# Three 256-column products into one half of PSUM instead of one of 512 and one of 256, in the feature-major tiles of a two-layer decoder trunk

## The chip, the cores and the metric

The kernel runs on one core of one Trainium2 chip. The metric is the device time of one execution in microseconds (us). Each profile is one execution recorded by the hardware profiler. In its rows PE is TensorE's products (matmuls), PEld TensorE's loads of the stationary operand, DVE is VectorE, ACT is ScalarE, POOL is GpSimd, SP is SyncE, whose queue (SPq) issues most of the DMAs.

## The reference

A trunk of two pre-norm layers over 256 tokens of width 2048, all in float32. Cut to its products:

```python
h = x                                             # 256 x 2048
h = h + chunked_gmlp(rmsnorm(h, a_norm), ...)     # u, v = gelu(xn @ w_in); (u * mix(v)) @ w_out
h = h + conv_ffn(rmsnorm(h, f_norm[0]), ...)      # up to 2 x 5632, causal conv of width 3, silu(gate) * val, down
k, v, c = fox_shared_kv(h, kv_norm, w_kvf, ...)   # keys, values, cumulative log forget gates
h = h + forgetting_attention(rmsnorm(h, b_norm), w_qg, ..., k, v, c)
h = h + conv_ffn(rmsnorm(h, f_norm[1]), ...)
return rmsnorm(h, final_norm)
```

The weights are some 400 MB, and each is used once. A norm's gain is multiplied into the activations ahead of a product; its scale for each token is multiplied in behind it.

## The kernel before

**Precision.** A float32 product is made of three products of the type float32r. Each weight chunk is split on the core into a high part (`whi`, a rounding copy on ScalarE, L82) and a low part (`wlo`, the difference, on VectorE, L83). Each activation tile is kept as a high part in columns 0 to 255 and a low part in columns 256 to 511 of one buffer (`X1`, `X2`, `H`; T is 256, the number of tokens). The kernel forms high × high, high × low and low × high, and leaves low × low out.

**The stream.** `Stream` holds a list of all weight chunks (128 × 1024 float32, 512 KB) in the order of the work. `run` (L86) goes through it once: at chunk i it issues the DMA of chunk i+6 on SyncE's queue (`_load`, L62, four `raw` buffers), the split of chunk i+3 (`_split`, L73, four `whi` and four `wlo` buffers), then the products of chunk i, and then one step of each evicting generator that has been started (`advance`, L57). This order is written by hand, and each engine works through its own instructions in it. So the instruction that reads a tile's sums stands on its engine ahead of the split of chunk i+4.

**Two kinds of chunks.** In token-major chunks (`tok_block`, L215: `a_in_v`, `b_q`, `kvf_k`, `kvf_v`) the activations are the stationary operand and the weights move, 512 columns a product. In feature-major chunks (`feat_block`, L168: `a_in_u`, `a_out`, `up0`, `down0`, `b_g`, `b_out`, `up1`, `down1`) the weights are stationary. A chunk holds four blocks kt of 128 input features (j from 0 to 3) by two blocks m of 128 output features, so eight weight tiles of 128 × 128 in a high and a low version. A tile of output is two blocks m by 256 tokens. It takes 4 chunks where the input has 2048 features (KD = 16 blocks) and 11 where it has 5632 (KF = 44 blocks, `down`).

**The wide form.** For each weight tile the high part meets all 512 columns of the activations at once, and its results stand in the two halves of one PSUM bank: high × high in columns 0 to T, high × low in T to 2T. The low part meets columns 0 to T and is added to the lower half:

```python
mm(ps[:, m, :], w, xx[:, kt, :], kt == 0, kt == K - 1)      # L187, high part
mm(ps[:, m, :T], w, xx[:, kt, :T], False, False)            # L189, low part
```

That is 16 products a chunk: first 8 wide ones, then 8 of 256 columns; in the last chunk of a tile the low ones come first. Every product goes with its own weight load. A tile has two PSUM banks (`main_ps`, L155, three such pairs in rotation).

**Eviction.** The two halves have to be added. `scaled_sum` (L296; used by `u_done`, `up_done` and `g_done`) copies the upper half on ScalarE (L299), adds it to the lower on VectorE (L300) and multiplies by the norm's scale (L301). `residual` (L303; behind `a_out`, `down0` and `b_out`) adds the lower half to h (L307), then the upper (L308). `final` (L332; behind `down1`) does so for each block m (L339, L340).

**The last tile.** The last tile of `down1` has a form of its own (`last_block`, L194): for each m, four low products, four high ones with the low activations and four high ones with the high activations, all of 256 columns and into the lower half of the bank, 24 products a chunk. `final_tile` (L317) is called behind each m of the last chunk.

**Around it.** Attention is spread as small products (L615, L616, L631, L638 to L640; 16 heads) between the chunks of `kvf_v` and `b_g`; in `a_in_u` the spatial mixing (L446) stands between tiles. L382 is a warm-up of TensorE ahead of the first chunk, nine products of one identity tile with itself.

Of the kernel before, what the change touches and what calls it, by code (L numbers as in the profile page):

```python
# [10 lines left out]
F32 = mybir.dt.float32  # L11
# [121 lines left out]
def build(ctx, tc, d, out):  # L133
# [21 lines left out]
    def main_ps():  # L155
        return psum.tile([P, 2, 512], F32, name="ps", tag="ps", bufs=3)
# [8 lines left out]
    def mm(o, a, b, start, stop):  # L165
        nc.tensor.matmul(o, a, b, start=start, stop=stop, skip_group_check=True)  # L166

    def feat_block(src, x, K, done, last=None):  # L168


        if last:
            return last_block(src, x, K, done, last)
        box = {}
        n = K // 4
        for c in range(n):
            def mult(hi, lo, c=c):
                if c == 0:
                    box["ps"] = main_ps()
                ps, xx = box["ps"], x()
                parts = (hi, lo) if c < n - 1 else (lo, hi)  # L180
                for i, part in enumerate(parts):
                    for j in range(4):
                        kt = 4 * c + j
                        for m in range(2):
                            w = part[:, j * 256 + m * P:j * 256 + (m + 1) * P]
                            if part is hi:
                                mm(ps[:, m, :], w, xx[:, kt, :], kt == 0, kt == K - 1)  # L187
                            else:
                                mm(ps[:, m, :T], w, xx[:, kt, :T], False, False)  # L189
                if c == n - 1:  # L190
                    s.start(done(ps))
            s.chunk(src[c], mult)

    def last_block(src, x, K, done, last):  # L194
        box = {}
        n = K // 4
        for c in range(n):
            def mult(hi, lo, c=c):
                if c == 0:
                    box["ps"] = main_ps()  # L200
                ps, xx = box["ps"], x()
                for m in range(2):
                    for part, half in ((lo, 0), (hi, 1), (hi, 0)):
                        for j in range(4):
                            kt = 4 * c + j
                            mm(ps[:, m, :T], part[:, j * 256 + m * P:j * 256 + (m + 1) * P],
                               xx[:, kt, half * T:(half + 1) * T], part is lo and kt == 0,
                               half == 0 and part is hi and kt == K - 1)
                    if c == n - 1:
                        last(ps, m)  # L210
                if c == n - 1:
                    s.start(done(ps))
            s.chunk(src[c], mult)

    def tok_block(src, x, done, load=None, prep=None):  # L215
# [77 lines left out]
            for i in range(2):  # L293
                nc.vector.tensor_tensor(acc, acc, sq[:, i, :], op=OP.add)

    def scaled_sum(ps, a):  # L296

        t = small.tile([P, 2, T], F32, name="half", tag="half", bufs=2)
        nc.scalar.activation(t, ps[:, :, T:], AF.Copy)  # L299
        nc.vector.tensor_tensor(a, ps[:, :, :T], t, op=OP.add)  # L300
        nc.vector.tensor_tensor(a, a, rB[:, None, :].to_broadcast([P, 2, T]), op=OP.mult)  # L301

    def residual(p, gain):  # L303

        def done(ps):
            hh = h[:, 2 * p:2 * p + 2, :]
            nc.vector.tensor_tensor(hh, hh, ps[:, :, :T], op=OP.add)  # L307
            nc.vector.tensor_tensor(hh, hh, ps[:, :, T:], op=OP.add)  # L308
            for kt in (2 * p, 2 * p + 1):
                prep(X1, kt, gain)  # L310
            square_into_acc(p)
            yield
            if p == 7:
                yield from token_scale()
        return done
# [15 lines left out]

    def final(p, gain):  # L332

        def done(ps):
            kts = (2 * p, 2 * p + 1)
            if p < 7:
                sq = small.tile([P, 2, T], F32, name="sq", tag="sq", bufs=2)
                for m, kt in enumerate(kts):
                    nc.vector.tensor_tensor(h[:, kt, :], h[:, kt, :], ps[:, m, :T], op=OP.add)  # L339
                    nc.vector.tensor_tensor(h[:, kt, :], h[:, kt, :], ps[:, m, T:], op=OP.add)  # L340
                    nc.scalar.activation(sq[:, m, :], h[:, kt, :], AF.Square)
                if p == 0:
                    nc.vector.tensor_tensor(acc, sq[:, 0, :], sq[:, 1, :], op=OP.add)
                else:
                    for i in range(2):
                        nc.vector.tensor_tensor(acc, acc, sq[:, i, :], op=OP.add)
            for kt in kts:
                nc.scalar.activation(h[:, kt, :], h[:, kt, :], AF.Copy, scale=column(gain + kt))
            if p == 5:
# [83 lines left out]
        return done  # L433

    def u_done(p):
        def done(ps):
            X2, vt, wT, bB, _ = mlp_kept()
            u = ph.temp("u", [P, 2, T])
            scaled_sum(ps, u)
            yield  # L440
            nc.scalar.activation(u, u, AF.Gelu)
            mp = misc_ps()
# [20 lines left out]
        return ph.keep("H", [P, KF, 2 * T], F32R)  # L463

    def up_done(l, i):
        def done(ps):
            state["layer"] = l
            H = ffn_h()
            a = ph.temp("a", [P, 2, T])
            scaled_sum(ps, a)  # L470
            yield
            c = ph.temp("c", [P, 2, T])
            for m in range(2):
# [14 lines left out]

    def ffn(l, done):
        for i in range(KF):  # L490
            feat_block(d[f"up{l}"][4 * i:4 * i + 4], lambda: X1, KD, up_done(l, i))
        for p in range(8):
            feat_block(d[f"down{l}"][11 * p:11 * p + 11], ffn_h, KF, done(p), final_tile if l and p == 7 else None)


    def att(key):
        ph.open("att")
        shape = {"X2": [P, KD, 2 * T], "q": [P, NH, T], "k": [P, NH, T], "v": [P, 2, D],
                 "ccol": [P, 2, NH]}[key]
        return ph.keep(key, shape, F32R if key == "X2" else F32)  # L500
# [151 lines left out]
            yield  # L652

    def g_done(p):
        def done(ps):
            X2, o = att("X2"), att("q")
            gg = ph.temp("big", [P, 512], bufs=6).rearrange("p (a b) -> p a b", a=2)
            scaled_sum(ps, gg)
# [31 lines left out]
        if blk == 1:  # L690
            s.then(at_load=load_mix)
    for p in range(8):
        feat_block(d["a_in_u"][4 * p:4 * p + 4], lambda: X1, KD, u_done(p))
    for p in range(8):
        feat_block(d["a_out"][4 * p:4 * p + 4], mlp_x2, KD, residual(p, C_FNORM))
    ffn(0, lambda p: residual(p, C_BNORM))

    s.then(at_mult=lambda: s.start(kv_operand()))
# [6 lines left out]
    for blk in range(4):  # L705
        tok_block(d["kvf_v"][8 * blk:8 * blk + 8], lambda: att("X2"), v_evict(blk))
    for p in range(8):
        feat_block(d["b_g"][4 * p:4 * p + 4], lambda: X1, KD, g_done(p))
    for p in range(8):
        feat_block(d["b_out"][4 * p:4 * p + 4], lambda: att("X2"), KD, residual(p, C_FNORM + KD))  # L710
    ffn(1, lambda p: final(p, C_FINAL))
    s.run()
    ph.close()
# [60 lines left out]
```

## Time and profile before

| | us |
|---|---|
| median of 3 runs | 2244.74 (2244.12 to 2244.78) |
| the profiled execution | 2244.26 |
| its span | 2242.6 |
| TensorE, products busy | 2228.1 (12,546 products) |
| TensorE, weight loads busy | 1927.1 (12,546 loads) |
| VectorE busy | 1528.5 |
| ScalarE busy | 1193.5 |
| DMA, queue of the weights | 56.7% of 16 engines' span |

The granted TensorE clock was 0.998 of full speed over the span. A row of a group reads: line, engine, operation, out<-in, shapes, count | busy us, mean ns of one | idle time of the engine before them, and what ended it. A product's row shows its way through the array, and the next product starts before it has ended, so the rate is read from the starts. In the order-of-time view like products in succession are one row: start, duration from the first start to the last end, engine, line, what, count, and in brackets what the engine waited for ahead of it.

### The profile page before, as it was taken

How to read it: one execution, taken by the hardware profiler on the slowest of the kernel's cores; microseconds unless marked ns; L12 is line 12 of the kernel's file. 1: busy time of each engine (PE TensorE's matmuls, PEld its weight loads, DVE VectorE, ACT ScalarE, POOL GpSimd, SP SyncE). 2: the span in 40 equal slices, each digit the busy share in tenths (PEclk: the TensorE clock that was granted, in tenths of full speed). 3: DMA queues.
4: the chain of work that ended last, by engine and by line, in shares of the span. 5: the costliest groups of instructions: out<-in, count | busy, mean ns of one | idle time of the engine just before them, and what ended most of it. 6: DMA issues, size and time to landing. Idle time of an engine off the chain costs nothing.

```text
span 2242.6 us, 32429 instructions
## 1 busy us (share of the span) xinstructions
PE 2228.1 (99%) x12546; PEld 1927.1 (86%) x12546; DVE 1528.5 (68%) x2219; ACT 1193.5 (53%) x1625; POOL 19.2 (1%) x41
## 2 busy tenths in 40 slices
PE   9999999999999999999999999999999999999998
PEld 7888888888888888888788888888888888888887
DVE  6566777777777755557786567677777777765554
ACT  6544455555555544445444666446555555544442
POOL 0000000000000000000000110000000000000000
PEclk9999999999999999999999999999999999999999
DMA  8555555656555555555555555555555555565553
GB/s 299 180 187 173 191 190 191 192 190 189 193 191 188 190 183 191 197 190 177 171 183 188 166 168 179 187 189 193 191 188 188 191 191 191 190 196 188 191 190 127
DMA packets 116443, 422.12 MB, mean 188 GB/s; under 512 B 13232, under 2 KB 13376, under 8 KB 116032
## 3 DMA queue, kind: packets, MB, share of 16 engines
q1 hardware_dynamic: 115344, 417.93, 56.7%
q0 software_dynamic: 768, 2.10, 0.3%
q8 instruction: 98, 1.61, 0.3%
q14 instruction: 57, 0.47, 0.1%
q10 hardware_dynamic: 176, 0.02, 0.0%
HBM read 417.88 MB, written 2.11 MB: 187 GB/s over the span
## 4 chain that ended last, share of the span: by engine, by line
PE 99%; DVE 0%; DMA 0%; ACT 0%; SPq 0%; DVEq 0%; issue 0%
PE ps L166 97%; PE mp L446 0%; PE mp L530 0%; PE mp L616 0%; DMA raw<-a_in_v 0%; PE mp L631 0%; PE mp L639 0%; PE mp L640 0%; PE mp L615 0%; PE mp L638 0%; DVE h L362 0%; PE mp L329 0%; PE mp L277 0%; DVE wlo L83 0%; DVEq L768 0%; ACT whi L82 0%
## 5 line engine op out<-in xcount | busy, mean ns | idle before, releaser
L83 DVE TENSOR_TENSOR wlo<-raw,whi 128x1024 fp32r<-128x1024 f32 (+1 forms) x786 | 953.3, 1221 | 378.8 <-ACT whi L82 377.3
L82 ACT ACTIVATE whi<-raw 128x1024 fp32r<-128x1024 f32 (+1 forms) x786 | 822.1, 1054 | 383.2 <-PE ps L166 353.9
L166 PE MATMUL ps<-X,whi 128*128 128x512 f32 x3328 | 829.6, 396 | 0.0
L166 PEld LDWEIGHTS ps<-X,whi 128*128 128x128 f32 x3328 | 602.7, 188 | 120.4
L166 PEld LDWEIGHTS ps<-X,wlo 128*128 128x128 f32 x3328 | 426.2, 188 | 28.1
L166 PE MATMUL ps<-X,wlo 128*128 128x256 f32 x3328 | 430.7, 277 | 0.0
L166 PE MATMUL ps<-ffn_H,whi 128*128 128x512 f32 (+1 forms) x1496 | 355.4, 381 | 0.0
L166 PEld LDWEIGHTS ps<-ffn_H,whi 128*128 128x128 f32 x1496 | 258.7, 188 | 45.3
L299 ACT ACTIVATE half<-ps 128x512 f32<-128x512 f32 x104 | 62.1, 597 | 256.1 <-PE ps L166 256.1
L166 PEld LDWEIGHTS ps<-ffn_H,wlo 128*128 128x128 f32 x1408 | 184.6, 188 | 13.8 <-DVE h L324 0.3
L166 PE MATMUL ps<-ffn_H,wlo 128*128 128x256 f32 x1408 | 188.5, 277 | 0.2 <-DVE h L324 0.2
L300 DVE TENSOR_TENSOR ffn_a<-ps,half 128x512 f32<-128x512 f32 x88 | 60.9, 692 | 175.1 <-ACT half L299 175.1
L166 PE MATMUL ps<-whi,att_X 128*128 128x512 f32 x512 | 168.1, 400 | 0.0
L480 DVE SCALAR_TENSOR_TENSOR ffn_c<-ffn_a,col,ffn_c 128x255 f32<-128x255 f32 x352 | 162.1, 481 | 6.3
L166 PE MATMUL ps<-whi,X 128*128 128x512 f32 x512 | 162.8, 395 | 0.9 <-ACT whi L82 0.9
L476 ACT ACTIVATE ffn_c<-ffn_a,col 128x256 f32<-128x256 f32 x176 | 96.4, 595 | 47.3 <-DVE ffn_a L301 47.3
L166 PEld LDWEIGHTS ps<-whi,X 128*128 128x128 f32 x512 | 96.2, 188 | 21.9 <-ACT whi L82 1.5
L166 PEld LDWEIGHTS ps<-whi,att_X 128*128 128x128 f32 x512 | 96.3, 188 | 20.4
L166 PE MATMUL ps<-wlo,X 128*128 128x512 f32 x256 | 99.7, 390 | 1.0 <-DVE wlo L83 1.0
L166 PE MATMUL ps<-wlo,att_X 128*128 128x512 f32 x256 | 100.0, 391 | 0.0
L245 ACT ACTIVATE X<-h,col 128x256 fp32r<-128x256 f32 x64 | 29.0, 500 | 101.8 <-DVE h L308 99.5
L250 ACT ACTIVATE ffn_H<-ffn_c 128x256 fp32r<-128x256 f32 x88 | 36.7, 418 | 70.2 <-DVE ffn_c L484 70.2
(147 smaller groups left out, 1215.0 us busy)
## 6 DMA issues: line engine op xcount, KB each, us to landing
raw<-up SPq DMA_DIRECT2D x352, 512.0 KB, 3.8
raw<-down SPq DMA_DIRECT2D x176, 512.0 KB, 4.2
raw<-a_in_u SPq DMA_DIRECT2D x32, 512.0 KB, 3.6
raw<-a_out SPq DMA_DIRECT2D x32, 512.0 KB, 4.3
raw<-b_q SPq DMA_DIRECT2D x32, 512.0 KB, 4.2
raw<-kvf_k SPq DMA_DIRECT2D x32, 512.0 KB, 4.0
raw<-kvf_v SPq DMA_DIRECT2D x32, 512.0 KB, 3.6
raw<-b_g SPq DMA_DIRECT2D x32, 512.0 KB, 3.3
```

Of the source, the lines that this page charges most:

```text
L82: self.nc.scalar.activation(hi[:, :n], raw, AF.Copy)
L83: self.nc.vector.tensor_tensor(lo[:, :n], raw, hi[:, :n].bitcast(F32), op=OP.subtract)
L166: nc.tensor.matmul(o, a, b, start=start, stop=stop, skip_group_check=True)
L245: nc.scalar.activation(dst[:, kt, :T], h[:, kt, :], AF.Copy, scale=g)
L250: nc.scalar.activation(dst[..., :T], src, AF.Copy)
L299: nc.scalar.activation(t, ps[:, :, T:], AF.Copy)
L300: nc.vector.tensor_tensor(a, ps[:, :, :T], t, op=OP.add)
L476: nc.scalar.activation(c[:, m, :], a[:, m, :], AF.Identity, scale=w[2], bias=column(C_CONVB + l * 2 * KF + f))
L480: nc.vector.scalar_tensor_tensor(c[:, m, n:], a[:, m, :T - n], w[k], c[:, m, n:], op0=OP.mult, op1=OP.add)
```

## The change

`feat_block` gets a second form, and a list `wide` for each tile of those of its chunks that keep the first form.

In the narrow form the high part meets the two halves of the activations in two products of 256 columns (`half` 0 and 1, one after the other with the same weight tile), and both are added into columns 0 to T of the bank; then come the low products as before. A chunk has 24 products with 24 weight loads. High products now come before low ones in every chunk. Where a tile has no wide chunk at all, the upper half of its banks isn't written, and the eviction is told so (`both` is false): `scaled` multiplies the lower half by the norm's scale straight out of PSUM, without the copy and the addition; `residual` and `final` leave out the second addition. Where a tile has a wide chunk, both halves are evicted; the copy of the upper half goes into the result's own buffer, and the buffer `half` is gone.

`last_block` is gone. The last tile of `down1` is now a narrow tile with `tile_done`: its last chunk is ordered by m, high before low, with `final_tile` behind each m; its other chunks have the order of all narrow ones.

These chunks keep the wide form: in `a_in_u` one of the four of each tile; the second chunk of the first tile of `a_out`; in each FFN the four of `up`'s first tile, one in each of its tiles 1, 9, 17, 25, 33 and 41, and one in each of the tiles 0 and 4 of `down`; all 32 of `b_g`; the first of `b_out`. That is 8 + 1 + 2 × 12 + 32 + 1 = 66. The feature-major chunks are 656 by the loops (the change's own description says 658). `final` squares both blocks of a tile in one instruction, by `square_into_acc`.

```diff
@@ -165,11 +165,10 @@
     def mm(o, a, b, start, stop):
         nc.tensor.matmul(o, a, b, start=start, stop=stop, skip_group_check=True)
 
-    def feat_block(src, x, K, done, last=None):
-
-
-        if last:
-            return last_block(src, x, K, done, last)
+    def feat_block(src, x, K, done, wide=(), tile_done=None):
+
+
+
         box = {}
         n = K // 4
         for c in range(n):
@@ -177,39 +176,36 @@
                 if c == 0:
                     box["ps"] = main_ps()
                 ps, xx = box["ps"], x()
-                parts = (hi, lo) if c < n - 1 else (lo, hi)
-                for i, part in enumerate(parts):
+
+                def product(part, half, j, m):
+                    kt = 4 * c + j
+                    w = part[:, j * 256 + m * P:j * 256 + (m + 1) * P]
+                    first = kt == 0 and part is hi and half in (None, 0)
+                    last = kt == K - 1 and part is lo
+                    if half is None:
+                        mm(ps[:, m, :], w, xx[:, kt, :], first, False)
+                    else:
+                        mm(ps[:, m, :T], w, xx[:, kt, half * T:(half + 1) * T], first, last)
+
+                halves = (None,) if c in wide else (0, 1)
+                if tile_done and c == n - 1:
+                    for m in range(2):
+                        for j in range(4):
+                            for half in halves:
+                                product(hi, half, j, m)
+                        for j in range(4):
+                            product(lo, 0, j, m)
+                        tile_done(ps, m)
+                else:
                     for j in range(4):
-                        kt = 4 * c + j
                         for m in range(2):
-                            w = part[:, j * 256 + m * P:j * 256 + (m + 1) * P]
-                            if part is hi:
-                                mm(ps[:, m, :], w, xx[:, kt, :], kt == 0, kt == K - 1)
-                            else:
-                                mm(ps[:, m, :T], w, xx[:, kt, :T], False, False)
+                            for half in halves:
+                                product(hi, half, j, m)
+                    for j in range(4):
+                        for m in range(2):
+                            product(lo, 0, j, m)
                 if c == n - 1:
-                    s.start(done(ps))
-            s.chunk(src[c], mult)
-
-    def last_block(src, x, K, done, last):
-        box = {}
-        n = K // 4
-        for c in range(n):
-            def mult(hi, lo, c=c):
-                if c == 0:
-                    box["ps"] = main_ps()
-                ps, xx = box["ps"], x()
-                for m in range(2):
-                    for part, half in ((lo, 0), (hi, 1), (hi, 0)):
-                        for j in range(4):
-                            kt = 4 * c + j
-                            mm(ps[:, m, :T], part[:, j * 256 + m * P:j * 256 + (m + 1) * P],
-                               xx[:, kt, half * T:(half + 1) * T], part is lo and kt == 0,
-                               half == 0 and part is hi and kt == K - 1)
-                    if c == n - 1:
-                        last(ps, m)
-                if c == n - 1:
-                    s.start(done(ps))
+                    s.start(done(ps, bool(wide)))
             s.chunk(src[c], mult)
 
     def tok_block(src, x, done, load=None, prep=None):
@@ -293,19 +289,22 @@
             for i in range(2):
                 nc.vector.tensor_tensor(acc, acc, sq[:, i, :], op=OP.add)
 
-    def scaled_sum(ps, a):
-
-        t = small.tile([P, 2, T], F32, name="half", tag="half", bufs=2)
-        nc.scalar.activation(t, ps[:, :, T:], AF.Copy)
-        nc.vector.tensor_tensor(a, ps[:, :, :T], t, op=OP.add)
-        nc.vector.tensor_tensor(a, a, rB[:, None, :].to_broadcast([P, 2, T]), op=OP.mult)
+    def scaled(ps, both, a):
+
+        src = ps[:, :, :T]
+        if both:
+            nc.scalar.activation(a, ps[:, :, T:], AF.Copy)
+            nc.vector.tensor_tensor(a, ps[:, :, :T], a, op=OP.add)
+            src = a
+        nc.vector.tensor_tensor(a, src, rB[:, None, :].to_broadcast([P, 2, T]), op=OP.mult)
 
     def residual(p, gain):
 
-        def done(ps):
+        def done(ps, both):
             hh = h[:, 2 * p:2 * p + 2, :]
             nc.vector.tensor_tensor(hh, hh, ps[:, :, :T], op=OP.add)
-            nc.vector.tensor_tensor(hh, hh, ps[:, :, T:], op=OP.add)
+            if both:
+                nc.vector.tensor_tensor(hh, hh, ps[:, :, T:], op=OP.add)
             for kt in (2 * p, 2 * p + 1):
                 prep(X1, kt, gain)
             square_into_acc(p)
@@ -331,19 +330,14 @@
 
     def final(p, gain):
 
-        def done(ps):
+        def done(ps, both):
             kts = (2 * p, 2 * p + 1)
             if p < 7:
-                sq = small.tile([P, 2, T], F32, name="sq", tag="sq", bufs=2)
-                for m, kt in enumerate(kts):
-                    nc.vector.tensor_tensor(h[:, kt, :], h[:, kt, :], ps[:, m, :T], op=OP.add)
-                    nc.vector.tensor_tensor(h[:, kt, :], h[:, kt, :], ps[:, m, T:], op=OP.add)
-                    nc.scalar.activation(sq[:, m, :], h[:, kt, :], AF.Square)
-                if p == 0:
-                    nc.vector.tensor_tensor(acc, sq[:, 0, :], sq[:, 1, :], op=OP.add)
-                else:
-                    for i in range(2):
-                        nc.vector.tensor_tensor(acc, acc, sq[:, i, :], op=OP.add)
+                hh = h[:, 2 * p:2 * p + 2, :]
+                nc.vector.tensor_tensor(hh, hh, ps[:, :, :T], op=OP.add)
+                if both:
+                    nc.vector.tensor_tensor(hh, hh, ps[:, :, T:], op=OP.add)
+                square_into_acc(p)
             for kt in kts:
                 nc.scalar.activation(h[:, kt, :], h[:, kt, :], AF.Copy, scale=column(gain + kt))
             if p == 5:
@@ -433,10 +427,10 @@
         return done
 
     def u_done(p):
-        def done(ps):
+        def done(ps, both):
             X2, vt, wT, bB, _ = mlp_kept()
             u = ph.temp("u", [P, 2, T])
-            scaled_sum(ps, u)
+            scaled(ps, both, u)
...
@@ -488,9 +482,11 @@
 
     def ffn(l, done):
         for i in range(KF):
-            feat_block(d[f"up{l}"][4 * i:4 * i + 4], lambda: X1, KD, up_done(l, i))
+            feat_block(d[f"up{l}"][4 * i:4 * i + 4], lambda: X1, KD, up_done(l, i),
+                       range(4) if i == 0 else (0,) if i % 8 == 1 else ())
         for p in range(8):
-            feat_block(d[f"down{l}"][11 * p:11 * p + 11], ffn_h, KF, done(p), final_tile if l and p == 7 else None)
+            feat_block(d[f"down{l}"][11 * p:11 * p + 11], ffn_h, KF, done(p), (0,) if p % 4 == 0 else (),
+                       final_tile if l and p == 7 else None)
 
 
     def att(key):
...
@@ -690,9 +686,9 @@
         if blk == 1:
             s.then(at_load=load_mix)
     for p in range(8):
-        feat_block(d["a_in_u"][4 * p:4 * p + 4], lambda: X1, KD, u_done(p))
+        feat_block(d["a_in_u"][4 * p:4 * p + 4], lambda: X1, KD, u_done(p), (1,) if p else (0,))
     for p in range(8):
-        feat_block(d["a_out"][4 * p:4 * p + 4], mlp_x2, KD, residual(p, C_FNORM))
+        feat_block(d["a_out"][4 * p:4 * p + 4], mlp_x2, KD, residual(p, C_FNORM), () if p else (1,))
     ffn(0, lambda p: residual(p, C_BNORM))
 
     s.then(at_mult=lambda: s.start(kv_operand()))
@@ -705,9 +701,9 @@
     for blk in range(4):
         tok_block(d["kvf_v"][8 * blk:8 * blk + 8], lambda: att("X2"), v_evict(blk))
     for p in range(8):
-        feat_block(d["b_g"][4 * p:4 * p + 4], lambda: X1, KD, g_done(p))
+        feat_block(d["b_g"][4 * p:4 * p + 4], lambda: X1, KD, g_done(p), range(4))
     for p in range(8):
-        feat_block(d["b_out"][4 * p:4 * p + 4], lambda: att("X2"), KD, residual(p, C_FNORM + KD))
+        feat_block(d["b_out"][4 * p:4 * p + 4], lambda: att("X2"), KD, residual(p, C_FNORM + KD), () if p else (0,))
     ffn(1, lambda p: final(p, C_FINAL))
     s.run()
     ph.close()
```

More of the change, by code (lines that the diff above doesn't have):

```diff
@@ L465, in up_done, with done @@
     def up_done(l, i):
-        def done(ps):
+        def done(ps, both):
             state["layer"] = l
@@ L469, in done @@
             a = ph.temp("a", [P, 2, T])
-            scaled_sum(ps, a)
+            scaled(ps, both, a)
             yield
@@ L654, in g_done, with done @@
     def g_done(p):
-        def done(ps):
+        def done(ps, both):
             X2, o = att("X2"), att("q")
             gg = ph.temp("big", [P, 512], bufs=6).rearrange("p (a b) -> p a b", a=2)
-            scaled_sum(ps, gg)
+            scaled(ps, both, gg)
             yield
```

## The prediction

> **What bounds the kernel now.** I read the head of the page first, then the chain that ended last, then TensorE's waits.
>
> ```profile
> span 2242.6 us, 32429 instructions
> PE 2228.1 (99%) x12546; PEld 1927.1 (86%) x12546; DVE 1528.5 (68%) x2219; ACT 1193.5 (53%) x1625; POOL 19.2 (1%) x41
> ...
> PE 99%; DVE 0%; DMA 0%; ACT 0%; SPq 0%; DVEq 0%; issue 0%
> ```
>
> ```profile
> PE mp L382 <- POOL ident L680: 1.5, 1, 1.5
> PE mp L277 <- DVE rcol L263: 1.3, 1, 1.3
> PE ps L166 <- DVE wlo L83: 1.0, 2, 0.8
> PE ps L166 <- ACT whi L82: 0.9, 2, 0.6
> PE mp L329 <- ACT sq L325: 0.6, 1, 0.6
> PE ps L166 <- DVE h L324: 0.2, 1, 0.2
> ```
>
> The chain is TensorE for 99% of the span, and all of TensorE's waits add up to 5.5 us. So the time is the sum of the spacings of the products, and an edit counts only by what it does to that spacing. A busy 99% doesn't say that the spacing is as short as it can be. For that I read one steady stretch in order of time. Columns: start, duration, what, count.
>
> ```profile
> 1961.77 3.89 PE L166 MATMUL ps<-X,whi 128*128 128x512 f32 x16
> ...
> 1972.86 3.89 PE L166 MATMUL ps<-X,whi 128*128 128x512 f32 x16
> ...
> 1982.14 1.98 PE L166 MATMUL ps<-X,wlo 128*128 128x256 f32 x16
> 1982.34 1.06 ACT L82 ACTIVATE whi<-raw 128x1024 fp32r<-128x1024 f32 x1 [0.48 <-PE ps L166]
> ...
> 1983.43 1.23 DVE L83 TENSOR_TENSOR wlo<-raw,whi 128x1024 fp32r<-128x1024 f32 x1 [0.55 <-ACT whi L82]
> ```
>
> From the first row to the second lies one tile of `up1`, four wide chunks: 11.09 us, or 2.7725 us a chunk. The mean row durations (396 ns for a product of 512, 277 for one of 256, by-form view below) are longer than the spacing, because products overlap. In a run of n the spacing is (duration of the run − duration of one) / (n − 1): (3.89 − 0.396)/15 = 232.9 ns for 512 columns, and (1.98 − 0.277)/15 = 113.5 ns for 256. Twice 113.5 is 227.0: two products of 256 columns take less than one of 512.
>
> The narrow form itself already runs in this kernel, in the last tile of `down1` (L194), with every product 256 wide and into one half of PSUM:
>
> ```profile
> 2199.36 0.62 PE L166 MATMUL ps<-ffn_H,wlo 128*128 128x256 f32 x4
> 2199.82 1.07 PE L166 MATMUL ps<-ffn_H,whi 128*128 128x256 f32 x8
> 2200.73 0.62 PE L166 MATMUL ps<-ffn_H,wlo 128*128 128x256 f32 x4
> ...
> 2226.57 0.62 PE L166 MATMUL ps<-ffn_H,wlo 128*128 128x256 f32 x4
> ```
>
> The pattern of 4 low and 8 high products is half a chunk. Twenty of them, ten chunks, lie between the first and the last row: 27.21 us, 2.721 us a chunk, 113.4 ns a product over 240 products.
>
> **The change part by part.**
>
> ```profile
> L82 ACT ACTIVATE whi<-raw 128x1024 fp32r<-128x1024 f32 (+1 forms) x786 | 822.1, 1054 | 383.2 <-PE ps L166 353.9
> ```
>
> Chunks. Each chunk has one high split. Of the 786, the loops make 129 token-major chunks and one for the forget gate, so 656 are feature-major.
>  Of these, 66 stay wide (8 in `a_in_u`, 1 in `a_out`, 12 in each FFN, 32 in `b_g`, 1 in `b_out`) and 11 are narrow already. So 579 chunks change form. They contain 579 × 8 = 4,632 wide products, each replaced by two, so there are 4,632 more products and as many more weight loads.
>
> The main term. 579 × (2.7725 − 2.721) = 579 × 0.0515 = **29.8 us saved**. The windows agree on the wide price:
>
> ```profile
> core 0: us, PE busy (x) PEld busy (x) DVE busy (x) ACT busy (x) POOL busy (x), PEclk, DMA share, GB/s
> 281.10:770.00 488.90, 488.90 (x2824) 425.89 (x2823) 372.66 (x537) 288.42 (x396) 0.00 (x0) 1.00 0.59 190
> 770.00:1014.00 244.00, 244.00 (x1409) 212.66 (x1408) 130.31 (x136) 102.68 (x113) 0.00 (x0) 1.00 0.57 191
> ...
> 2199.00:2227.00 28.00, 28.00 (x247) 27.91 (x246) 12.07 (x14) 9.92 (x12) 0.00 (x0) 1.00 0.29 96
> ```
>
> `down0` is 88 chunks in 244.00 us, 2.773 each. The last window shows what is different about the narrow stretch: the loader is busy 27.91 of 28 us, against 87% in the wide stages, DMA is at half its share, and VectorE at 43% against 76% in `up0`. So the narrow form leaves the weight loader no slack, and I have seen it only beside light work. Against a dependence on that work: the sixteen low products at 1982.14 ran at 113.5 ns while a high split and a low split ran beside them in `up1`. Bounds of this term: at 113.5 a chunk is 2.724 us and the gain 28.1 us; at the loader's spacing in a run of eight below, (0.98 − 0.188)/7 = 113.1, it is 2.714 and 33.9 us.
>
> ```profile
> 2199.71 0.98 PEld L166 LDWEIGHTS ps<-ffn_H,whi 128*128 128x128 f32 x8
> ...
> L166 PE MATMUL ps<-X,whi 128*128 128x512 f32 x3328 | 829.6, 396 | 0.0
> L166 PE MATMUL ps<-X,wlo 128*128 128x256 f32 x3328 | 430.7, 277 | 0.0
> ...
> L166 PE MATMUL ps<-mlp_X,whi 128*128 128x512 f32 x256 | 63.8, 396 | 0.0
> ...
> L166 PEld LDWEIGHTS ps<-X,whi 128*128 128x128 f32 x3328 | 602.7, 188 | 120.4
> ```
>
> One rule speaks against this term. The Trainium skill, "TensorE: Matmul & The Clock Gate", section "Back-to-back issue gap", gives a warm gap of N/2.4 + 2.5 ns, so a fixed toll on each product; by it 512 columns take 215.8 ns, twice 256 take 218.3, and the change would cost an estimated 4,632 × 2.5 = 11.6 us. The rows above disagree with it at 512 columns, where they have 232.9. The same page's section "LDWEIGHTS (loading the stationary operand)" gives 128/1.2 = 106.7 ns for a load, which would put loader and product of 256 columns at nearly the same limit; the full loader of the last window agrees.
>
> The same weights twice. What the last tile doesn't show is the new order: halves 0 and 1 of one weight tile in direct succession, where L194 goes through four weight tiles first. The nearest rows with one stationary tile twice in a row are a head's products: L638 and L639 both hold the first block of v, L640 the second.
>
> ```profile
> 1257.28 0.38 PE L638 MATMUL mp<-att_pT,att_v 128*128 128x128 f32 x2
> 1257.50 0.39 PE L639 MATMUL mp<-att_pT,att_v 128*128 128x128 f32 x2
> 1257.72 0.39 PE L640 MATMUL mp<-att_pT,att_v 128*128 128x128 f32 x2
> ...
> 1261.37 0.49 PE L631 MATMUL mp<-ident,att_big 128*128 128x128 f32 x3
> ...
> 1.46 3.98 PE L382 MATMUL mp<-ident 128*128 128x128 f32 x18 [1.46 <-POOL ident L680]
> ```
>
> ```profile
> L631 PE MATMUL mp<-ident,att_big 128*128 128x128 f32 x48 | 7.8, 272 | 0.0
> ...
> L382 PE MATMUL mp<-ident 128*128 128x128 f32 x18 | 4.0, 414 | 1.5 <-POOL ident L680 1.5
> ```
>
> Each step is 0.22 us, with the same weights or others, so I take nothing for it. The other end is the warm-up at L382, nine products of one tile: (3.98 − 0.41)/17 = 210 ns a record (0.41 us is one record's own duration), against (0.49 − 0.272)/2 = 109 for the three different tiles of L631. It is the first work of the run, when much else is unlike the steady state.
>
> Instruction supply. TensorE's instructions come over this queue:
>
> ```profile
> q8 instruction: 98, 1.61, 0.3%
> ```
>
> 1.61 MB for 12,546 pairs is 128 B a pair, so 4,632 pairs are some 36 fetches more. The last tile uses about two in its 264 pairs and has no gap between its regular rows. I take nothing.
>
> Eviction. In 74 of the 104 scaled tiles ScalarE's copy (L299) and VectorE's add (L300) go; in 25 residual and final tiles the second add goes; 7 final tiles take wider instructions.
>
> ```profile
> L299 ACT ACTIVATE half<-ps 128x512 f32<-128x512 f32 x104 | 62.1, 597 | 256.1 <-PE ps L166 256.1
> ...
> L300 DVE TENSOR_TENSOR ffn_a<-ps,half 128x512 f32<-128x512 f32 x88 | 60.9, 692 | 175.1 <-ACT half L299 175.1
> ```
>
> That is 74 × 0.597 = 44 us of ScalarE and 74 × 0.692 = 51 us of VectorE, all behind TensorE, so worth nothing now. The new wait: VectorE's scaling reads the sum directly, so it waits for TensorE instead of for ScalarE. Behind it in VectorE's queue is the low split of the chunk four further on, which TensorE needs three chunks (8 us) later; it already sat there behind L300. The high splits wait for TensorE (353.9 us), not TensorE for them. If that cover were gone, each tile would pay at most the 0.69 us of the scaling.
>
> Order in a tile's last chunk (high before low), start and stop flags, the smaller memory: nothing. The low part is ready, or the waits would show it; products on operands at different places, X and mlp_X, have the same mean of 396 ns. The tail behind the last chunk issues what it issued.
>
> The sum: the profiled execution took 2244.26 us, 1.66 more than its span, and 0.48 less than the median of the three runs. 2244.26 − 29.8 = **2214.5 us**. Its own range, from the bounds of the main term with some 3 us for the unseen order at tile ends, is 2208 to 2219.
>
> **The rivals.**
>
> 1. *A start toll on each product.* Products have a fixed cost beside their columns, and halving them adds it. For it: the token-major products, all 512 wide, are a little closer than the feature-major ones, so spacing depends on what stands beside a product.
>
> ```profile
> 11.14 43.99 PE ps L166 x191
> ```
>
> 43.99/191 = 230.3 against 232.9, 2.6 ns. If a further product costs that, 4,632 × 2.6 = 12.0 us more: 2256.3 us, slower. The rule above is this rival with 2.5 ns. It decides from 115.5 ns a product (2.7725/24), 2.1 above the last tile's. Against it: 240 products at 113.4.
>
> 2. *The second load of a tile is not hidden.* If the loader can't run ahead while the array holds the same tile, eight products a chunk pay the warm-up's excess of 101 ns: 579 × 8 × 0.101 = 468 us, 2712 us. From 6.4 ns each the change loses (0.0515/8). Against it: L638 and L639.
>
> 3. *Supply becomes the bound.* If splits or weights come no faster than one chunk in 2.77 us, the gain stays on paper: 2244 us, the second load filling idle time. For it: VectorE's 76% in `up0`. Against it: VectorE also loses work there, and TensorE waited for splits 1.9 us in all, in four waits.
>
> 4. *The second load is skipped or shortened.* Then the eight repeated products come at the closest spacing that the rows show, 109 ns, and a chunk saves 8 × 4.4 = 35 ns more: 20 us, 2194 us. Against it: L639 was no closer behind L638 than L640 behind L639, and the loader's count equals the products' (12,546 each).
>
> **How the numbers follow.** Forecast 0.80, toll 0.06, second load 0.04, supply 0.05, skipped load 0.05. The predicted time is the forecast's, 2214.5. Its own 2208 to 2219 widened by some way towards the skipped load and towards a supply that takes part of the gain gives 2205 to 2226, which leaves out the whole of rivals 1 and 2 and most of 3 and 4. Faster by over 0.2% (4.5 us, about what a measurement of this kernel can tell from no change): the forecast, the skipped load and a third of the supply case, 0.87. Within: the rest of the supply case, 0.03. Slower: 0.10.
>
> **What would show each step.** Narrow chunks of the FFN 2.72 us apart and 113 ns a product: the main term. Half 1 of a weight tile later than half 0 by more than 116 ns: rival 2, and shorter than 112: rival 4. Low and high products equally at 116 or more: rival 1. Waits of L166 for splits: rival 3. `b_g` must keep its time, since all of it stays wide, and so must the token-major stages. The prediction is wrong if narrow chunks in a stage with full load traffic are over 2.73 us apart.

## The result, and the profile after

| | before | after |
|---|---|---|
| median, us | 2244.51 (2244.12 to 2244.78, 4 runs) | 2213.93 (2213.61 to 2215.5, 4 runs) |
| ratio | 1 | 0.9865, 95% interval 0.9848 to 0.9882 |
| profiled execution, us | 2244.26 | 2214.11 |
| its span, us | 2242.6 | 2212.4 |

The forecast was 2214.5 us. The lines of the page after that answer to those shown of before, busy time and counts by engine and the instruction queue:

```profile
span 2212.4 us, 41566 instructions
...
PE 2197.1 (99%) x17178; PEld 2103.3 (95%) x17178; DVE 1467.5 (66%) x2106; ACT 1151.1 (52%) x1544; POOL 19.0 (1%) x41
...
q8 instruction: 134, 2.20, 0.4%
...
PE 99%; DMA 0%; DVE 0%; ACT 0%; SPq 0%; DVEq 0%; issue 0%
```

There are 4,632 more products and loads (17,178 − 12,546) and 36 more instruction fetches (134 − 98), and TensorE is still the whole chain. Its waits after the change (who waited for whom; us in all, times, longest):

```profile
PE ps L166 <- ACT whi L82: 1.7, 2, 1.2
...
PE ps L166 <- DVE wlo L83: 1.0, 2, 0.8
```

Neither split became a bound. A steady stretch of `up0` in order of time, and a window over most of that stage (PE busy, PEld busy, VectorE, ScalarE, POOL, clock, DMA share, GB/s):

```profile
500.67 1.98 PE L166 MATMUL ps<-X,whi 128*128 128x256 f32 x16
502.48 1.07 PE L166 MATMUL ps<-X,wlo 128*128 128x256 f32 x8
503.39 1.98 PE L166 MATMUL ps<-X,whi 128*128 128x256 f32 x16
...
508.83 1.98 PE L166 MATMUL ps<-X,whi 128*128 128x256 f32 x16
```

```profile
280.00:760.00 480.00, 480.00 (x4152) 476.45 (x4151) 350.08 (x501) 268.21 (x361) 0.00 (x0) 1.00 0.60 194
```

Three chunks lie between 500.67 and 508.83: 2.720 us each, 113.3 ns a product, where the prediction had 2.721. The loader is busy 99% of this window, beside a DMA share of 0.60. By the starts of each stage's first product in the two traces, `up0` lost 8.9 us, `down0` 4.6, `up1` 8.9, `down1` with the last tile 3.7, `a_in_u` 1.3, `a_out` 1.7, `b_out` 1.7, and 0.3 lies ahead of the first product. `b_g`, all wide, kept its 99.5, and the token-major stages theirs, except that `a_in_v` took 0.9 us more (91.7). Together that is the 30.2 us of the span. `a_in_v`, the first stage, takes 90.7 to 93.9 us in the traces whose kernels leave its products alone, so its 0.9 us says nothing of the change.

### The profile page after: what moved, and what is told of

Its sections match the earlier page's. It is cut to its first block, busy times and chain, and to the rows that moved or that the text cites. A ratio compares the mean times of both kernels' runs of the same rounds, so it can differ in the third digit from the quotient of the medians.

```text
span 2212.4 us, 41566 instructions
## 1 busy us (share of the span) xinstructions
PE 2197.1 (99%) x17178; PEld 2103.3 (95%) x17178; DVE 1467.5 (66%) x2106; ACT 1151.1 (52%) x1544; POOL 19.0 (1%) x41
## 4 chain that ended last, share of the span: by engine, by line
PE 99%; DMA 0%; DVE 0%; ACT 0%; SPq 0%; DVEq 0%; issue 0%
PE ps L166 97%; PE mp L440 0%; PE mp L526 0%; PE mp L612 0%; DMA raw<-a_in_v 0%; PE mp L627 0%; PE mp L635 0%; PE mp L636 0%; PE mp L611 0%; PE mp L634 0%; DVE h L356 0%; PE mp L328 0%; PE mp L273 0%; DVE wlo L83 0%; DVEq L764 0%; ACT whi L82 0%
## 5 line engine op out<-in xcount | busy, mean ns | idle before, releaser
L166 PE MATMUL ps<-X,whi 128*128 128x256 f32 (+1 forms) x6176 | 828.0, 286 | 0.0
L166 PEld LDWEIGHTS ps<-X,whi 128*128 128x128 f32 x6176 | 758.4, 188 | 16.4
L166 PE MATMUL ps<-X,wlo 128*128 128x256 f32 x3328 | 445.7, 277 | 0.0
L166 PEld LDWEIGHTS ps<-X,wlo 128*128 128x128 f32 x3328 | 413.2, 188 | 5.4
L166 PE MATMUL ps<-ffn_H,whi 128*128 128x256 f32 (+1 forms) x2784 | 348.3, 278 | 0.2 <-DVE h L323 0.2
L166 PEld LDWEIGHTS ps<-ffn_H,whi 128*128 128x128 f32 x2784 | 330.5, 188 | 1.3 <-DVE h L323 0.3
L166 PEld LDWEIGHTS ps<-ffn_H,wlo 128*128 128x128 f32 x1408 | 173.0, 188 | 0.4
L299 DVE TENSOR_TENSOR ffn_a<-ps,rB 128x512 f32<-128x512 f32 x74 | 51.2, 691 | 96.7 <-PE ps L166 96.7
L166 PE MATMUL ps<-att_X,whi 128*128 128x256 f32 (+2 forms) x520 | 68.9, 282 | 0.0
L166 PEld LDWEIGHTS ps<-att_X,whi 128*128 128x128 f32 (+1 forms) x520 | 61.5, 185 | 2.2
```

What stands on the lines that cost most here:

```text
L299: nc.vector.tensor_tensor(a, src, rB[:, None, :].to_broadcast([P, 2, T]), op=OP.mult)
```

## The experiments

Ratios are to the kernel before, run beside each. Eleven kernels ran; all stand here.

**Does the eviction count?** `e3_wide_less_evict` is the kernel before with its wide products, and with the upper halves not evicted.

```diff
-        nc.scalar.activation(t, ps[:, :, T:], AF.Copy)
-        nc.vector.tensor_tensor(a, ps[:, :, :T], t, op=OP.add)
-        nc.vector.tensor_tensor(a, a, rB[...], op=OP.mult)
+        nc.vector.tensor_tensor(a, ps[:, :, :T], rB[...], op=OP.mult)
...
-            nc.vector.tensor_tensor(hh, hh, ps[:, :, T:], op=OP.add)
...
```

> The products of the kernel before, but no tile evicts its upper half: the high x low sums are left out of the output, ScalarE's copy and VectorE's additions are gone. Theory A: no change, 2244 us within 2 us. Rival C: a share of the 30 us, at half of it 2229 us.

Measured: 2244.57 us, ratio 1.0 (0.9991 to 1.001). VectorE's busy time fell from 1528.5 to 1454.3 us and ScalarE's from 1193.5 to 1131.0, and the end didn't move. Theory A holds here.

**Does a repeated weight tile count?** `e4_apart` reorders the changed kernel's high products.

```diff
-                    for j in range(4):
-                        for m in range(2):
-                            for half in halves:
+                    for half in halves:
+                        for j in range(4):
+                            for m in range(2):
                                 product(hi, half, j, m)
```

> The changed kernel with the high products of a narrow chunk in another order: half 0 of all eight weight tiles, then half 1 of all eight, so no tile is loaded twice in succession (the last chunk of the last tile excepted). Theory A: the same, 2214 us within 2 us, 113.4 ns a product. Rival D (a repeated tile costs or saves something): if a repeat saved 4.4 ns, 8 x 570 x 0.0044 = 20 us slower than the changed kernel, 2234 us; if it cost as much, 2194 us.

Measured: 2213.82 us, ratio 0.9865 (0.9851 to 0.988), the changed kernel's time, and `up0` took 479.96 us against 479.97. A repeat costs nothing and saves nothing.

**What do the 66 wide chunks do?** `e1_all_narrow` gives them the narrow form too.

```diff
-                halves = (None,) if c in wide else (0, 1)
+                halves = (0, 1)
...
-                    s.start(done(ps, bool(wide)))
+                    s.start(done(ps, False))
```

> All 656 feature-major chunks take the narrow form, no tile evicts an upper half. Theory A (only the spacing of the products counts, 113.4 ns for 256 columns against 232.9 for 512): the 66 chunks give 66 x 0.0515 = 3.4 us more, 2210.5 us, ratio to before 0.985. Rival B (the wide chunks stand where they let the splits or the attention's small products catch up): the stages with wide chunks get no shorter, or waits for splits appear in b_g, 2214 us or more.

Measured: 2267.63 us (2266.29 to 2268.69), ratio 1.0103 (1.0088 to 1.0118). That is slower than both kernels, 54 us over the changed one, for 66 chunks of 656. Theory A missed, and so did rival B's mechanism: TensorE waited 1.5 us for high and 1.0 us for low splits, and `b_g` got shorter, 98.5 us. The order of time around the start of the first FFN shows what happened:

```profile
283.03 1.98 PE L166 MATMUL ps<-X,whi 128*128 128x256 f32 x16
284.85 1.07 PE L166 MATMUL ps<-X,wlo 128*128 128x256 f32 x8
285.76 0.50 PE L328 MATMUL mp<-ones,acc 128*128 128x1 f32 x4
286.12 2.13 PE L166 MATMUL ps<-X,whi 128*128 128x256 f32 x16
288.08 1.11 PE L166 MATMUL ps<-X,wlo 128*128 128x256 f32 x8
289.02 2.05 PE L166 MATMUL ps<-X,whi 128*128 128x256 f32 x16
...
501.25 2.05 PE L166 MATMUL ps<-X,whi 128*128 128x256 f32 x16
...
1939.73 2.05 PE L166 MATMUL ps<-X,whi 128*128 128x256 f32 x16
...
1942.56 2.05 PE L166 MATMUL ps<-X,whi 128*128 128x256 f32 x16
```

```profile
300.00:780.00 480.00, 480.00 (x4078) 480.00 (x4077) 331.96 (x466) 252.50 (x340) 0.00 (x0) 1.00 0.57 187
```

Ahead of the token sums (L328, four records of one column each) sixteen products take 1.98 us, behind them 2.05, and still so 215 us later; the second FFN is the same. A chunk takes 1942.56 − 1939.73 = 2.83 us there, 117.9 ns a product, more than the 2.7725 us of the wide form. The window over most of `up0` has a granted clock of 1.00, as it had in the changed kernel, so the clock isn't the reason. So products of 256 columns have two steady spacings, 113.4 and some 117.8 ns, and a row of narrow chunks stays in the one it is in as long as no other products come between. Both FFNs ran slow throughout, 54.5 us in all over the changed kernel; the other feature-major stages came out 1.5 us shorter than there.

**Is it the half of PSUM?** `e2_two_halves` cuts all high products to 256 columns, but leaves the second of each in the upper half, with the eviction of both. (The last tile keeps the changed kernel's form.)

```diff
-                        mm(ps[:, m, :T], w, xx[:, kt, half * T:(half + 1) * T], first, last)
+                        up = half if both else 0
+                        mm(ps[:, m, up * T:(up + 1) * T], w, xx[:, kt, half * T:(half + 1) * T], first, last)
...
```

> All high products are 256 columns wide, but the second of each pair goes into the upper half of the bank as before, and every tile except the last evicts both halves as before. Theory A (spacing of the products only): as with all chunks narrow, 2210.5 us. Rival C (part of the gain comes from one half of PSUM, or from the eviction that is left out): nearer to 2244 us; half of the gain lost would be 2229 us.

Measured: 2267.61 us, ratio 1.0107 (1.009 to 1.0124). The number of A missed with `e1_all_narrow`, by the slow spacing; against that run it is the right comparison, and the two are equal, FFN by FFN. So the place of the sums and the shorter eviction count for nothing at the slow spacing. `a_out` and `b_out` ran at the fast spacing in both kernels and took the same there too, 87.95 and 87.04 us. So, with `e3_wide_less_evict`, nothing of the gain is theirs.

**What switches to the slow spacing?** `e9_no_token_products` is `e1_all_narrow` without the token sums and the norm scale ahead of the two FFNs.

```diff
-            if p == 7:
+            if p == 7 and gain == C_BNORM:
                 yield from token_scale()
```

> All chunks narrow, and the token sums ahead of the two FFNs are left out (the six small TensorE products and the norm scale that they give; the scale of the stage before is used). Theory E: nothing switches the spacing there, so both FFNs run at 113.4 ns if the stage ahead of them did: 2267.6 - 54.6 = 2213 us, 2 us less with the products themselves. Rival G (the FFNs are slow because of their operands or of the load traffic in them): 2266 us.

Measured: 2210.34 us, ratio 0.985 (0.9835 to 0.9865). All chunks are narrow, and both FFNs are fast from end to end (order of time, the same place):

```profile
283.52 1.98 PE L166 MATMUL ps<-X,whi 128*128 128x256 f32 x16
285.33 1.07 PE L166 MATMUL ps<-X,wlo 128*128 128x256 f32 x8
286.24 1.98 PE L166 MATMUL ps<-X,whi 128*128 128x256 f32 x16
```

Operands, load traffic and the length of the row are the same as in `e1_all_narrow`, so rival G falls. The norm scale's work on the other engines goes with the token sums; that the products are what switches is read from the order of time of `e1_all_narrow`, where the spacing changes at them.

**How few wide chunks are enough?** Four kernels differ from `e1_all_narrow` only in which chunks of `up` are wide, in each FFN.

```diff
# e7_first_tile_only
+                       range(4) if i == 0 else ())
# e8_one_later_chunk
+                       (0,) if i == 1 else ())
# e10_two_later_chunks
+                       range(2) if i == 1 else ())
# e11_chunk_behind
+                       (3,) if i == 0 else ())
```

> All chunks narrow except the four of up's first tile in each FFN (8 of 656). Theory E (256-column products have two steady spacings, 113.4 and 117.7 ns; small products between them, the token sums ahead of an FFN above all, switch to the slow one; wide products behind them switch back, and it then stays): both FFNs at 113.4, so the run with all chunks narrow less 54.6 us in the FFNs, and 2 us less than the changed kernel elsewhere: 2212 us. Rival F (the slow spacing sets in by itself in a long row of narrow chunks, and the wide chunk in every eighth tile keeps it off): up to 20 us a layer of up come back, 2230 to 2265 us.

Measured: 2211.4 us (2211.1 to 2211.43), ratio 0.9854 (0.9837 to 0.987). Both FFNs ran at the fast spacing to their ends, the second for over 700 us without a further wide chunk (order of time, the place of the row at 1939.73 above):

```profile
1940.71 1.98 PE L166 MATMUL ps<-X,whi 128*128 128x256 f32 x16
1942.53 1.07 PE L166 MATMUL ps<-X,wlo 128*128 128x256 f32 x8
```

So rival F falls: the wide chunks in every eighth tile of `up` and in `down` weren't needed here.

> All chunks narrow except one, the first chunk of up's second tile, in each FFN (2 of 656). Theory E with one wide chunk being enough: slow only for the four or five chunks ahead of it, (4 or 5) x 24 x 0.0044 = 0.5 us a layer: 2212 to 2213 us. Theory E with more than one needed: both FFNs stay at 117.7 ns, 2267 us.

Measured: 2266.49 us, ratio 1.0101 (1.0086 to 1.0116). One wide chunk changes nothing, though it stands directly behind the two transposes of the token scale (L273):

```profile
291.84 0.38 PE L273 MATMUL mp<-ident,rcol 128*128 128x128 f32 x2
291.98 2.11 PE L166 MATMUL ps<-X,whi 128*128 128x512 f32 x8
293.92 1.11 PE L166 MATMUL ps<-X,wlo 128*128 128x256 f32 x8
294.86 2.05 PE L166 MATMUL ps<-X,whi 128*128 128x256 f32 x16
```

> All chunks narrow except the first two of up's second tile in each FFN (4 of 656), where one alone left both FFNs slow. Theory J (in the changed kernel the low products behind the first wide chunk are still at 118 ns and those behind the second at 113, so a second wide chunk in succession brings the fast spacing back): 2212 us. Rival K (no wide product brings it back once the spacing is slow; the wide chunks protect only where they stand directly behind the small products): 2266 us.

Measured: 2211.27 us in one run. Two in succession bring the fast spacing back, from a slow one that had lasted since L328:

```profile
289.93 0.38 PE L273 MATMUL mp<-ident,rcol 128*128 128x128 f32 x2
290.07 2.11 PE L166 MATMUL ps<-X,whi 128*128 128x512 f32 x8
292.01 1.10 PE L166 MATMUL ps<-X,wlo 128*128 128x256 f32 x8
292.95 2.03 PE L166 MATMUL ps<-X,whi 128*128 128x512 f32 x8
294.82 1.08 PE L166 MATMUL ps<-X,wlo 128*128 128x256 f32 x8
295.74 1.98 PE L166 MATMUL ps<-X,whi 128*128 128x256 f32 x16
```

The low runs of eight tell it: 1.10 us behind the first wide chunk, 1.08 behind the second, 1.98 for the sixteen that follow. In the second FFN it was the same. Rival K falls.

> All chunks narrow except one, the last of up's first tile in each FFN, which stands directly behind the two transposes of the token scale. Rival K (protects where it stands directly behind the small products): slow for two or three chunks only, 2212 us. Theory J (two in succession are needed from the slow state): 2266 us.

Measured: 2266.02 us in one run, as theory J has it. The expectation misplaced the chunk: it came out directly ahead of the transposes, not behind them. So this run is a second single wide chunk that doesn't help; the place behind them is what `e8_one_later_chunk` tried.

**Why 256 columns?** `e5_widths` cuts the 512 columns elsewhere, by stage.

```diff
+                            for a, b in zip(cuts, cuts[1:]):
+                                mm(ps[:, m, a:b], w, xx[:, kt, a:b], kt == 0 and a == 0, False)
...
```

> The changed kernel, with the 512 columns of each high product cut in other places, into both halves: a_out 384+128, b_out 320+192, down0 four times 128, the first four tiles of down1 448+64. Theory H (a product can't follow the last one sooner than its weight load, 113 ns; above it a column costs 0.455 ns): pairs take 288, 259, 4 x 113 and 317 ns; a_out 103 us (changed kernel 88), b_out 95 (87), down0 398 (239). Rival I (columns alone count): each as two of 256, no stage longer by over 2 us.

Measured, one run: 2426.06 us; `a_out` 102.9 us, `b_out` 95.2, `down0` 395.4. Rows of it from `a_out`, `down0` and `down1` (a pair of unequal products stands in one row, under the first one's shape):

```profile
199.94 2.39 PE L166 MATMUL ps<-mlp_X,whi 128*128 128x384 f32 x16
202.17 1.12 PE L166 MATMUL ps<-mlp_X,wlo 128*128 128x256 f32 x8
203.13 2.39 PE L166 MATMUL ps<-mlp_X,whi 128*128 128x384 f32 x16
...
901.32 3.69 PE L166 MATMUL ps<-ffn_H,whi 128*128 128x128 f32 x32
904.84 1.14 PE L166 MATMUL ps<-ffn_H,wlo 128*128 128x256 f32 x8
905.81 3.69 PE L166 MATMUL ps<-ffn_H,whi 128*128 128x128 f32 x32
...
2139.68 2.60 PE L166 MATMUL ps<-ffn_H,whi 128*128 128x448 f32 x16
2142.11 1.18 PE L166 MATMUL ps<-ffn_H,wlo 128*128 128x256 f32 x8
2143.13 2.60 PE L166 MATMUL ps<-ffn_H,whi 128*128 128x448 f32 x16
```

Products of unequal width are read from whole chunks, since the first start of a row comes early and the low products behind it come late. Less eight low products of 113.4 ns, the chunk of 203.13 − 199.94 = 3.19 us leaves 285 ns for a pair of 384 and 128 columns, the one of 4.49 us 112 ns for each product of 128, and the one of 3.45 us 318 ns for a pair of 448 and 64; by its stage time, a pair of 320 and 192 in `b_out` takes 258 ns. Two of 256 take 227. Theory H had 288, 113, 317 and 259, and rival I, 227 for each pair, falls. So there is a floor of some 112 ns a product. That it is the weight load is argued, since no run changes the length of a load, and single starts don't follow H's words: in the row at 199.94 the next product starts some 58 ns behind one of 128 columns, and the one after that 227 ns later. The Trainium skill, "TensorE: Matmul & The Clock Gate", section "LDWEIGHTS (loading the stationary operand)", gives 128/1.2 = 106.7 ns for a load, and the 112 ns lie 5% above it. At 256 columns the columns' time has come down to about that floor: at H's 0.455 ns a column, 256 of them are 116.5 ns, and the row has 113.4.

**A version that goes further?** `e12_token_major_too` is `e7_first_tile_only` with the token-major products halved too.

```diff
-                        mm(ps[:, tb, :], a, hi[:, w], kt == 0, False)
-                        mm(ps[:, tb, :], a, lo[:, w], False, False)
-                        mm(ps[:, tb, :], b, hi[:, w], False, kt == KD - 1)
+                        for x_, w_ in ((a, hi), (a, lo), (b, hi)):
+                            for q in range(2):
...
```

> The version with only up's first tile wide (2211.4 us), and the token-major products cut into two of 256 columns as well (129 chunks, 24 products each). At 113.4 ns a token-major chunk takes 2.72 us where twelve of 512 take 12 x 229.6 = 2.755: 4.4 us less, 2207 us. At 117.7 ns it takes 2.825: 9 us more, 2220 us. Theory E (small products switch the spacing) expects a mixture in the stages with transposes and heads, 2207 to 2220 us, and the fast spacing in no stage for certain.

Measured: 2224.75 us (2218.81 to 2227.38), ratio 0.9904 (0.9887 to 0.992). That is slower than its base, and the median lies above the 2207 to 2220 us that were expected. In the profiled run (2227.38 us, the slowest of the four) `a_in_v` ran slow from its first products, and this carried on through `a_in_u` and `a_out`, where no wide product is left: 4.3, 3.3 and 3.4 us more than in its base, and 1.4 to 2.1 more in each of `b_q`, `kvf_k` and `kvf_v`. Of the 4.3 us the slow spacing explains 32 × (2.825 − 2.755) = 2.2; the rest is within what `a_in_v` varies by from run to run.

## Why the prediction came out right, and what it missed

**The main term** was right, in its size (29.8 us forecast, 30.2 in the span) and in each of its prices: wide chunk 2.7725, narrow chunk 2.720 to 2.721, 579 chunks. Shown by the rows of after and by `e9_no_token_products`, where both FFNs run narrow chunks alone at the same spacing.

**Eviction, PSUM half, repeated weights, order, instruction supply at nothing**: right. The first three are shown by `e3_wide_less_evict`, `e2_two_halves` against `e1_all_narrow`, and `e4_apart`; for order and supply there are the waits for splits (2.7 us, 1.9 before) and the 36 fetches alone. Rivals 2 and 4 fall with `e4_apart`, rival 3 with the waits.

**Two readings were weaker than they looked.** The prediction took the loader's 27.91 of 28 us to mean that the narrow form leaves it no slack. Loads of 188 ns that start 113 ns apart overlap, so the loader shows as busy throughout at any spacing under 188 ns, and the full row says nothing of a limit, nor does it bear out the 106.7 ns that it was set beside; `e5_widths` is what bears on that. And the rule that it took from the Trainium skill, "TensorE: Matmul & The Clock Gate", section "Back-to-back issue gap", is given there for an isolated product. An estimate by it is 109.2 ns for 256 columns, and the rows of after have 113.3.

**What it missed** is in the step that took one spacing for the narrow form. "Against it: 240 products at 113.4" was set against a toll as if 113.4 ns belonged to the width. It belongs to a state, and there is a second, at 117.8, beyond the 115.5 from which the change loses. Rival 1 had the right threshold and a wrong mechanism: the toll isn't paid on each product, but by a whole row of them once small products have put it there. Had the change been made in all 656 chunks, the prediction's arithmetic would have given 2211 us and the chip takes 2268. The 66 wide chunks were counted as chunks that gain nothing. Eight of them (the first tile of `up` in each FFN, by `e7_first_tile_only`) hold the gain of the 579. So the price of a narrow chunk was worked out, but that the chunks would keep it was luck: the prediction had no reason to count on the wide chunks for it.

The trace of before showed this state to whoever compared rows of one kind. Behind the token sums of the second FFN stands this row (order of time, kernel before), 16 low products as in the row at 1982.14 that the prediction quoted:

```profile
1504.83 2.05 PE L166 MATMUL ps<-X,wlo 128*128 128x256 f32 x16
...
1510.67 1.07 PE L166 MATMUL ps<-X,wlo 128*128 128x256 f32 x8
```

Here they take 2.05 us, there 1.98: (2.05 − 0.277)/15 = 118.2 ns. The next low row is fast again, (1.07 − 0.277)/7 = 113.3 ns, with two rows of wide products and the two transposes of the token scale between. In the wide form it costs some 5 ns on the 16 low products of two chunks, nothing that shows in the time.

**Open.** Why there are two states and not one isn't settled. That load floor and columns' time nearly meet at 256 columns (`e5_widths`) makes it plausible that the row can lock in two ways; that is argued, not shown. Nor is it shown why two wide chunks in succession bring the fast one back and one doesn't, or whether a shorter row of wide products would. Which small products switch isn't fixed by their kind: in `e1_all_narrow` the token sums switched both FFNs, while in the changed kernel those of the last tile left the row fast, and the groups of the spatial mixing in `a_in_u` all did. Small products brought the fast spacing back, too. `b_g` of `e1_all_narrow` has no wide product, and there the spacing changes with the attention heads:

```profile
1321.27 2.24 PE L166 MATMUL ps<-X,whi 128*128 128x256 f32 x16
1323.34 1.11 PE L166 MATMUL ps<-X,wlo 128*128 128x256 f32 x8
1324.29 0.49 PE L627 MATMUL mp<-ident,att_big 128*128 128x128 f32 x3
1324.53 2.07 PE L166 MATMUL ps<-X,whi 128*128 128x256 f32 x16
1326.44 1.07 PE L166 MATMUL ps<-X,wlo 128*128 128x256 f32 x8
```

The low row ahead of a head's three transposes (L627) is slow and the one behind them fast, six times out of seven. The two transposes of the token scale (L273) left the FFNs slow in the same run. What makes the difference isn't shown.

The fastest version tried, `e7_first_tile_only` with 8 wide chunks, took 2211.1 to 2211.43 us against the changed kernel's 2213.61 to 2215.5. These were not timed beside each other and lie 0.1% apart, which is less than a comparison of this kernel can tell for certain; the stages show where it is, 1.0 us of it in `b_g`.

## What to carry to other kernels

Where TensorE is the whole chain, read the spacing of its products from runs of n in order of time, for each shape and in each stage, and compare rows of one kind: a difference of 4% between two such rows was a state here, and it decided more than the difference between forms. The mean of such a row by shape shows it as well: 281 ns in `e1_all_narrow`, 276 or 277 in `e7_first_tile_only`. Look for the width below which a product no longer gets cheaper, which here is 256 columns, and cut no narrower; next to that width the row may have a slower way to run. After an interruption by small products, check which of the two it is in, and try a few wide products behind them if it is the slow one; here two chunks of them were enough and one was not.

## What the runs showed of the hardware that was not expected

- A row of float32r products of 256 columns with a weight load each runs at 113.4 or at 117.8 ns a product at a granted clock of 1.00, and kept either for a whole FFN (some 700 us).
- A few small products switched it from the fast to the slow (the token sums ahead of both FFNs) or from the slow to the fast (three transposes of a head in `b_g` of `e1_all_narrow`); two chunks of wide products in succession switched it back (2211.27 us), one did not (2266.49, 2266.02).
- A product of 512 columns takes 233 ns, 6 more than two of 256 at the fast spacing. A narrower product than 256 saves almost nothing: 112 ns at 128 columns.
